# Experts of at most 64 rows: rounded rows and rests side by side in one stationary

## The chip, the cores and the metric

The kernel runs on one core of one Trainium2 chip. The metric is device time in microseconds (us), the median of three runs. Inside the core TensorE (PE) multiplies, VectorE (DVE) and ScalarE (ACT) work element by element, GpSimd (POOL) does small steps and issues the gathers and scatters, and SyncE (SP) issues nearly all other transfers (DMA).

## The reference

One layer of a hybrid encoder over 1024 tokens of width 1024: a modulated norm, a wide projection, three mixers (convolution, neighbourhood attention, a gated delta rule in both directions), an output projection, then a mixture of 32 experts, and a final norm. The change touches only the experts. Cut to what matters there:

```python
gate = pg_top * jax.nn.softmax(top_logit, axis=-1)          # two experts per token
expert = (grp[:, None] * EXPERTS_PER_GROUP + top_e).reshape(-1)
...
def expert_block(args):
    xb, e = args                                            # the rows that chose expert e
    return (jax.nn.silu(xb @ w1[e]) * (xb @ w3[e])) @ w2[e]  # 1024 -> 512, 512 -> 1024
...
ys = ys * gate...                                           # weighted, and added to the token
x = x + gate2 * y_moe
return _rmsnorm(x, final_norm_w)
```

All of it is fp32. Each expert has three weight matrices of 2 MiB each, 6 MiB together; 2048 rows (1024 tokens, two experts each) are spread unevenly over the 32 experts.

## The kernel before

**Products.** PE runs its fast fp32r form, which rounds its operands, so each fp32 operand is held as a rounded part and a rest: `split` (line 61) is one copy on ACT (the rounded part, `wh`, `xh`, `uh`) and one subtraction on DVE (the rest, `wl`, `xl`, `ul`). A product of two such operands is three matmuls in `mm3` (line 1351): rounded by rounded, rest by rounded, rounded by rest. The expert's rows are the stationary operand (128 deep, as wide as there are rows), the weights are the moving one (128 deep, 512 columns).

**Places.** The experts are ranked by size on the chip, but for the first three, which stand where they are. `ROOM` (line 30) says how many rows the expert of each rank can have; what goes beyond it is done by a loop behind the straight code (line 1611), which runs as many passes as are needed, none here. The 32 experts are taken in a fixed order of places; rank r is called a column in the code. Columns 3 and 4 (192 rows) are taken at places 18 and 24 (`TWICE`), as two blocks of 128 and 64 rows that share the weights; column 5 is at place 3, column 14 at place 12, column 19 at place 17, column 20 at place 19, column 25 at place 25, column 31 at place 31. The rooms give 128 rows at places 0 to 9, 96 at 10 to 13, 80 at 14 to 17, 64 at 19 to 23, 25 and 26, and 48 at 27 to 31. So there are 34 blocks.

**One place.** `hidden` (line 1504) makes the two hidden products: for w1 and then w3, for two halves g of the depth, it takes one weight tile of 1 MiB, split in two pieces of 128x1024 (`chunk_split`, line 1268, three buffers each for `wh` and `wl`), and runs 12 matmuls: 48 in all, in two accumulators `h1` and `h3`. `gated` (line 1382) applies Silu to the first on ACT and multiplies by the second on DVE (`u`). `prep_x` (line 1499) prepares the next place's rows: eight PE transposes into two banks `pt`, each split in `xh` and `xl`, and the gather of a later block. `output` (line 1519) multiplies the place before with its w2: 24 matmuls, two multiplications by gate and modulation into `yo` on DVE, and the scatter that adds the rows to `x2_d` (POOL). Last, `t` (line 1389) turns `u` with four PE transposes and splits it in `uh` and `ul` for the next place's turn. So a place costs 72 matmuls and 12 splits of weights. Each engine runs its instructions in order; the compiler puts them in an order of its own, near this one.

**Weights.** 192 loads of 1 MiB go through 16 buffers in order, issued by SP as buffers come free (`weights`, line 1528; `load_tile`, line 1175), with at most four in flight.

**Other lines.** `slots_of` (line 1439) finds the rows of the second blocks of columns 3 and 4, once, at place 5: 16 times DVE makes a matrix `q` (line 1455, one buffer of its own) which PE multiplies (line 1456). The last two blocks skip the scatter: their rows are put side by side (line 1558), and `out_on_chip` (line 1422) and `last` (line 1584) add them on the chip, apply the final norm and store. Line 1149 is the router's product and line 1037 one of its index steps, both true fp32 products; line 1145 is an ACT copy of a 128x512 bank.

Of the kernel before, what the change touches and what calls it, by code (L numbers as in the profile page):

```python
# [8 lines left out]
F32 = mybir.dt.float32  # L9
F32R = mybir.dt.float32r  # L10
I32 = mybir.dt.int32
AF = mybir.ActivationFunctionType
# [4 lines left out]
P = 128  # L17
# [3 lines left out]
KT = D // P  # L21
# [5 lines left out]
TWICE = (18, 24)  # L27
LATE = 5
FEATS = (*range(0, 1280, P), *range(1536, 3072, P))
ROOM = ((3, 128), (5, 192), (12, 128), (16, 96), (20, 80), (27, 64), (32, 48))  # L30


def body(tc, I, O):
# [5 lines left out]
def _body(ctx, tc, nc, I, O):  # L39
    pe, act, dve, pool, sp = nc.tensor, nc.scalar, nc.vector, nc.gpsimd, nc.sync  # L40
# [8 lines left out]
    ident = const.tile([P, P], F32, name="ident")  # L49
# [188 lines left out]
    for i in range(2):  # L238
        acc = st.tile([P, D], F32, name=f"acc{i}")
        for k in range(KT):  # L240
# [3 lines left out]
            w = st.tile([P, D], F32, name="wa", bufs=4)  # L244
# [1106 lines left out]
    def mm3(out, xh, xl, k0, w, first, last):  # L1351
        n = 0
        for k in range(4):
            wh, wl = w[k // 2]
            for a, b in ((xh, wh), (xl, wh), (xh, wl)):
                pe.matmul(out, a[:, k0 + k], b[:, k % 2], start=first and n == 0, stop=last and n == 11)  # L1356
                n += 1

    class Block:


        def __init__(self, i, idx, n=P):
            self.n = n
            self.xg, self.idx, self.yo = xgs[i % 3][:n], lambda: [x[:n] for x in idx()], None

        def gather(self):
            return pool.indirect_dma_start(out=self.xg, out_offset=None, in_=xn_d,  # L1367
# [2 lines left out]

        def x(self):
            n = self.n
            xh = ex.tile([P, KT, P], F32R, name="xh")[:, :, :n]
            xl = ex.tile([P, KT, P], F32R, name="xl")[:, :, :n]
            for g in range(2):
                pt = pse.tile([P, 4, P], F32, name="pt", bufs=2)[:, :, :n]
                for j in range(4):
                    pe.transpose(pt[:, j], self.xg[:, (4 * g + j) * P:(4 * g + j + 1) * P], ident[:n, :n])  # L1378
                split(xh[:, 4 * g:4 * g + 4], xl[:, 4 * g:4 * g + 4], pt)
            self.xs = xh, xl  # L1380

        def gated(self, n):
            if n:
                self.yo = ex.tile([P, D], F32, name="yo", bufs=2)[:self.n]
            u = self.u = self.yo[:, :512] if n else ex.tile([P, 512], F32, name="u", bufs=1)[:self.n]
            act.activation(u, self.hs[0], AF.Silu)
            dve.tensor_mul(u, self.hs[1], u)

        def t(self, n=0):
            m = self.n  # L1390
            pt = pse.tile([P, 4, P], F32, name="ut")[:, :, :m]
            for j in range(4):
                pe.transpose(pt[:, j], self.u[:, j * P:(j + 1) * P], ident[:m, :m])
            uh = ex.tile([P, 4, P >> n], F32R, name=f"uh{n}", bufs=1)[:, :, :m]
            ul = ex.tile([P, 4, P >> n], F32R, name=f"ul{n}", bufs=1)[:, :, :m]
            split(uh, ul, pt)
            self.us = uh, ul
# [41 lines left out]
    def slots_of(ebs, ob):  # L1439


        m = len(ebs)
        pb = ex.tile([P, 2, NT], F32, name="pb", bufs=1)
        dve.tensor_scalar(pb, pos, ob, None, op0=OP.add)
        sl = ex.tile([P, NT, 2, 2, 2], F32, name="sl", bufs=1)[:, :, :, :m]
        on = ex.tile([P, NT, 2], F32, name="on", bufs=1)
        for i, eb in enumerate(ebs):
            dve.tensor_scalar(on, eid, eb, None, op0=OP.is_equal)
            dve.tensor_mul(sl[:, :, :, i], slot, on[:, :, :, None].to_broadcast([P, NT, 2, 2]))
        tabo = pse.tile([P, 512], F32, name="tab")[:, :2 * m]  # L1450
        n = 0
        for t in range(NT):
            for a in range(2):
                q = ex.tile([P, P], F32, name="q", bufs=1)
                dve.tensor_scalar(q, iota, pb[:, a, t:t + 1], None, op0=OP.is_equal)
                pe.matmul(tabo, q, sl[:, t, a].rearrange("p i k -> p (i k)"), start=n == 0, stop=n == 2 * NT - 1)
                n += 1
        tb = small.tile([P, 2, 2], F32, name="tb")[:, :m]
        dve.tensor_copy(tb, tabo.rearrange("p (i k) -> p i k", k=2))
        ix1 = small.tile([P, 2], I32, name="ix1")[:, :m]  # L1460
        indices(small, tb[:, :, 0], ix1, m)
        return [(ix1[:, i:i + 1], tb[:, i, 1:2], tb[:, i, 0:1]) for i in range(m)]
# [41 lines left out]
    def hidden(bs, weights, between=iter(())):  # L1504

        for b in bs:
            b.hs = []
        for nms in (("h1", "tab"), ("h3", "y")):
            for b, nm in zip(bs, nms):
                b.hs.append(pse.tile([P, 512], F32, name=nm, bufs=2 if nm == "y" else 1)[:b.n])  # L1510
            for g in range(2):
                next(between, None)
                w = weights()
                for b in bs:
                    mm3(b.hs[-1], *b.xs, 4 * g, w, g == 0, g == 1)
        for n, b in enumerate(bs):
            b.gated(n)

# [19 lines left out]
    g = blks[0].gather()  # L1538
# [340 lines left out]
```

## Time and profile before

| | us |
|---|---|
| median of three runs | 1533.52 |
| lowest and highest run | 1529.77, 1535.05 |
| profiled execution | 1529.12 |
| span of the profile | 1527.3 |
| stretch of the experts (first hidden matmul to last) | 872.3 to 1479.5 |

Line numbers below are those of the kernel before. A matmul's time in the profile is its latency, since matmuls are pipelined; what one costs PE is the distance from start to start. On DVE and ACT, too, a short overlap of neighbours makes distances shorter than times. The busy share of an engine says how near it is to its limit in a stretch; the releaser named behind idle time says what ended a wait. PEclk is the granted clock of TensorE as a share of 2.4 GHz.

### The profile page before, as it was taken

What the parts mean: (1) busy time and instruction counts of PE and PEld (TensorE: products, weight loads), DVE (VectorE), ACT (ScalarE), POOL (GpSimd) and SP (SyncE); (2) the same over time, 40 slices, a digit from 0 to 9 for tenths busy, and PEclk for the clock granted to TensorE, in tenths of its full rate; (3) what the DMA queues carried; (4) which work ended last, traced back from release to release, by engine and by line L of the source; (5) the groups of instructions that cost most, each with busy time, mean ns of one, the idle gap of its engine ahead of it and who ended that gap; (6) DMA issues with size and microseconds to landing.
All of it is one profiled execution on the core that took longest, in us unless ns stands there. A gap on an engine that the chain in (4) does not pass through costs nothing. (4 is left out here: it accounts for less than half of the span.)

```text
span 1527.3 us, 21968 instructions
## 1 busy us (share of the span) xinstructions
PE 1380.7 (90%) x7319; PEld 1054.2 (69%) x7319; DVE 1185.0 (78%) x2148; ACT 792.4 (52%) x1293; POOL 380.9 (25%) x294
## 2 busy tenths in 40 slices
PE   3987999999877898879999699999999999999994
PEld 3865777777665888878887578787766665665542
DVE  6758766554647688867788799999999789878995
ACT  3633554433444322322322288787777567657773
POOL 0011321100101555633432111221244113212222
PEclk9999999999999999999999599999999999999997
DMA  9496455224778665677566699999999999979832
GB/s 338 120 200 195 143 183 165 88 75 96 204 208 208 187 202 181 203 252 238 207 207 226 255 335 374 346 381 364 351 374 370 363 337 371 334 271 339 322 111 117
DMA packets 172601, 375.75 MB, mean 246 GB/s; under 512 B 33458, under 2 KB 99634, under 8 KB 147908
## 3 DMA queue, kind: packets, MB, share of 16 engines
q1 hardware_dynamic: 162500, 351.13, 67.2%
q0 software_dynamic: 7072, 16.73, 4.6%
q10 hardware_dynamic: 2912, 6.46, 1.4%
q8 instruction: 59, 0.97, 0.3%
q14 instruction: 58, 0.48, 0.1%
HBM read 325.31 MB, written 56.87 MB: 250 GB/s over the span
## 5 line engine op out<-in xcount | busy, mean ns | idle before, releaser
L61 DVE TENSOR_TENSOR wl<-w,wh 128x1024 fp32r<-128x1024 f32 (+1 forms) x392 | 460.6, 1196 | 44.8 <-ACT wh L61 39.7
L61 ACT CAST wh<-w 128x1024 fp32r<-128x1024 f32 (+1 forms) x392 | 403.9, 1033 | 161.2 <-PE y L1356 69.1
L1356 PE MATMUL h<-wl,xh 128*128 128x512 f32 (+4 forms) x512 | 204.1, 399 | 0.4 <-DVE wl L61 0.3
L1356 PE MATMUL h<-wh,xh 128*128 128x512 f32 (+4 forms) x512 | 204.4, 399 | 0.1
L1356 PE MATMUL h<-wh,xl 128*128 128x512 f32 (+4 forms) x512 | 202.0, 394 | 0.6 <-DVE xl L61 0.6
L1408 POOL DMA_INDIRECT x_d<-yo,ixp x27 | 100.0, 3703 | 198.6 <-DVE yo L1404 184.1
L339 PE MATMUL mm<-hh,wh 128*128 128x512 f32 x352 | 148.1, 421 | 0.0
L339 PE MATMUL mm<-hh,wl 128*128 128x512 f32 x352 | 143.0, 406 | 1.9 <-DVE wl L61 1.9
L339 PE MATMUL mm<-hl,wh 128*128 128x512 f32 x352 | 142.6, 405 | 0.0
L1356 PE MATMUL y<-wh,uh 128*128 128x512 f32 (+4 forms) x272 | 108.8, 401 | 1.1 <-ACT uh L61 1.1
L1356 PE MATMUL y<-wl,uh 128*128 128x512 f32 (+4 forms) x272 | 108.1, 398 | 0.1
L1356 PE MATMUL y<-wh,ul 128*128 128x512 f32 (+4 forms) x272 | 106.9, 394 | 0.5 <-DVE ul L61 0.5
L1356 PEld LDWEIGHTS h<-wl,xh 128*128 128x128 f32 (+4 forms) x512 | 80.9, 158 | 36.8 <-DVE wl L61 2.0
L1356 PEld LDWEIGHTS h<-wh,xl 128*128 128x128 f32 (+4 forms) x512 | 81.0, 158 | 36.7 <-DVE xl L61 1.4
L1356 PEld LDWEIGHTS h<-wh,xh 128*128 128x128 f32 (+4 forms) x512 | 81.1, 158 | 34.2 <-ACT wh L61 0.7
L1367 POOL DMA_INDIRECT oacc<-xn_d,ixp x29 | 35.2, 1213 | 211.4 <-PE pt L1378 195.5
L339 PEld LDWEIGHTS mm<-hh,wh 128*128 128x128 f32 x352 | 68.1, 193 | 18.5 <-issue 7.0
L339 PEld LDWEIGHTS mm<-hl,wh 128*128 128x128 f32 x352 | 67.7, 192 | 15.5 <-issue 0.3
L339 PEld LDWEIGHTS mm<-hh,wl 128*128 128x128 f32 x352 | 68.1, 193 | 13.9 <-DVE wl L61 2.2
L404 POOL TENSOR_TENSOR acc<-acc,wa 128x512 f32<-128x512 f32 x28 | 41.1, 1466 | 86.3 <-ACT wa L402 47.8
L1356 PEld LDWEIGHTS y<-wl,uh 128*128 128x128 f32 (+4 forms) x272 | 42.5, 156 | 21.2 <-DVE wl L61 2.2
L1356 PEld LDWEIGHTS y<-wh,uh 128*128 128x128 f32 (+4 forms) x272 | 42.4, 156 | 19.4 <-ACT uh L61 1.6
(433 smaller groups left out, 2893.3 us busy)
## 6 DMA issues: line engine op xcount, KB each, us to landing
w<-we SPq DMA_DIRECT2D x192, 1024.0 KB
wa<-w_ada SPq DMA_DIRECT2D x64, 256.0 KB
wa<-w_ada SPq DMA_DIRECT2D x16, 512.0 KB
wr<-w_in_f SPq DMA_DIRECT2D x16, 512.0 KB
qkv_d<-t SPq DMA_DIRECT2D x12, 512.0 KB
f<-qkv_d SPq DMA_DIRECT2D x8, 768.0 KB
t_d<-zt SPq DMA_DIRECT2D x8, 516.0 KB
xt<-x SPq DMA_DIRECT2D x8, 512.0 KB
```

Source lines behind the costliest of these rows:

```text
L61: return act.copy(hi, src), dve.tensor_sub(lo, src, hi.bitcast(F32))
L339: pe.matmul(ps, a[:, k], of(b, k, h * 512, 512), start=n == 0, stop=n == 3 * KT - 1)
L404: pool.tensor_add(acc, acc, w)
L1356: pe.matmul(out, a[:, k0 + k], b[:, k % 2], start=first and n == 0, stop=last and n == 11)
L1367: return pool.indirect_dma_start(out=self.xg, out_offset=None, in_=xn_d, in_offset=bass.IndirectOffsetOnAxis(ap=self.idx()[0], axis=0), bo ...
L1408: return pool.indirect_dma_start(out=x2_d, out_offset=bass.IndirectOffsetOnAxis(ap=self.idx()[0], axis=0), in_=self.yo, in_offset=None, bo ...
```

## The change

Blocks of at most 64 rows (`both`) are computed in another way. `ROOM` now has 128 rows at places 0 to 11 and 64 at places 12 to 17, 19 to 23 and 25 to 31, so with the second blocks of places 18 and 24 there are 20 such blocks. Their rounded rows stand in columns 0 to 63 of `xh` and their rests in columns 64 to 127, as one stationary 128 wide; `mm2` multiplies it by `wh` and by `wl`, two matmuls where `mm3` has three. The accumulators then have 128 rows, of which row r and row r + 64 are to be added. `gated` only copies the two accumulators to SBUF (two ACT copies of 128x512, in a buffer of `xl`). `t` has eight true fp32 matmuls with `fold`, a 128x64 matrix of two identities above each other, which add the halves and turn the result in one step, four for each accumulator; then Silu (ACT, 128x256), the multiplication (DVE, 128x256) and the split follow on the turned rows. `su`, which holds the first two results, takes the one buffer `u`. `q` of `slots_of` takes that buffer too and loses its own.

```diff
--- before.py
+++ after.py
@@ -27,7 +27,8 @@
 TWICE = (18, 24)
 LATE = 5
 FEATS = (*range(0, 1280, P), *range(1536, 3072, P))
-ROOM = ((3, 128), (5, 192), (12, 128), (16, 96), (20, 80), (27, 64), (32, 48))
+ROOM = ((3, 128), (5, 192), (14, 128), (32, 64))
+HALF = P // 2
 
 
 def body(tc, I, O):
@@ -1356,12 +1357,25 @@
                 pe.matmul(out, a[:, k0 + k], b[:, k % 2], start=first and n == 0, stop=last and n == 11)
                 n += 1
 
+    fold = ex.tile([P, HALF], F32, name="fold", bufs=1)
+    dve.tensor_add(fold, ident[:, :HALF], ident[:, HALF:])
+
+    def mm2(out, xs, k0, w, first, last):
+
+        n = 0
+        for k in range(4):
+            for b in w[k // 2]:
+                pe.matmul(out, xs[:, k0 + k], b[:, k % 2], start=first and n == 0, stop=last and n == 7)
+                n += 1
+
     class Block:
+
 
 
         def __init__(self, i, idx, n=P):
             self.n = n
             self.xg, self.idx, self.yo = xgs[i % 3][:n], lambda: [x[:n] for x in idx()], None
+            self.both = n <= HALF
 
         def gather(self):
             return pool.indirect_dma_start(out=self.xg, out_offset=None, in_=xn_d,
@@ -1370,16 +1384,28 @@
 
         def x(self):
             n = self.n
-            xh = ex.tile([P, KT, P], F32R, name="xh")[:, :, :n]
-            xl = ex.tile([P, KT, P], F32R, name="xl")[:, :, :n]
+            xh = ex.tile([P, KT, P], F32R, name="xh")
+            if self.both:
+                self.xs = xh
+                xh, xl = xh[:, :, :n], xh[:, :, HALF:HALF + n]
+            else:
+                xh, xl = xh[:, :, :n], ex.tile([P, KT, P], F32R, name="xl")[:, :, :n]
+                self.xs = xh, xl
             for g in range(2):
                 pt = pse.tile([P, 4, P], F32, name="pt", bufs=2)[:, :, :n]
                 for j in range(4):
                     pe.transpose(pt[:, j], self.xg[:, (4 * g + j) * P:(4 * g + j + 1) * P], ident[:n, :n])
                 split(xh[:, 4 * g:4 * g + 4], xl[:, 4 * g:4 * g + 4], pt)
-            self.xs = xh, xl
+
+        def hidden(self, w, g):
+            (mm2 if self.both else mm3)(self.hs[-1], *((self.xs,) if self.both else self.xs), 4 * g, w, g == 0, g == 1)
 
         def gated(self, n):
+            if self.both:
+                self.hc = ex.tile([P, KT, P], F32, name="xl").rearrange("p (i k) f -> p i k f", i=2)
+                for i in range(2):
+                    act.copy(self.hc[:, i].rearrange("p k f -> p (k f)"), self.hs[i])
+                return
             if n:
                 self.yo = ex.tile([P, D], F32, name="yo", bufs=2)[:self.n]
             u = self.u = self.yo[:, :512] if n else ex.tile([P, 512], F32, name="u", bufs=1)[:self.n]
@@ -1388,9 +1414,20 @@
 
         def t(self, n=0):
             m = self.n
-            pt = pse.tile([P, 4, P], F32, name="ut")[:, :, :m]
-            for j in range(4):
-                pe.transpose(pt[:, j], self.u[:, j * P:(j + 1) * P], ident[:m, :m])
+            pt = pse.tile([P, 4, P], F32, name="ut")
+            if self.both:
+                ht = pt.rearrange("p k (i f) -> p i k f", i=2)
+                for i in range(2):
+                    for j in range(4):
+                        pe.matmul(ht[:, i, j], self.hc[:, i, j], fold, start=True, stop=True)
+                su = ex.tile([P, 512], F32, name="u", bufs=1).rearrange("p (i k f) -> p i k f", i=2, k=4)
+                act.activation(su[:, 0], ht[:, 0], AF.Silu)
+                dve.tensor_mul(su[:, 1], ht[:, 1], su[:, 0])
+                pt = su[:, 1][:, :, :m]
+            else:
+                pt = pt[:, :, :m]
+                for j in range(4):
+                    pe.transpose(pt[:, j], self.u[:, j * P:(j + 1) * P], ident[:m, :m])
             uh = ex.tile([P, 4, P >> n], F32R, name=f"uh{n}", bufs=1)[:, :, :m]
             ul = ex.tile([P, 4, P >> n], F32R, name=f"ul{n}", bufs=1)[:, :, :m]
             split(uh, ul, pt)
@@ -1451,7 +1488,7 @@
         n = 0
         for t in range(NT):
             for a in range(2):
-                q = ex.tile([P, P], F32, name="q", bufs=1)
+                q = ex.tile([P, 512], F32, name="u", bufs=1)[:, :P]
                 dve.tensor_scalar(q, iota, pb[:, a, t:t + 1], None, op0=OP.is_equal)
                 pe.matmul(tabo, q, sl[:, t, a].rearrange("p i k -> p (i k)"), start=n == 0, stop=n == 2 * NT - 1)
                 n += 1
@@ -1507,12 +1544,12 @@
             b.hs = []
         for nms in (("h1", "tab"), ("h3", "y")):
             for b, nm in zip(bs, nms):
-                b.hs.append(pse.tile([P, 512], F32, name=nm, bufs=2 if nm == "y" else 1)[:b.n])
+                b.hs.append(pse.tile([P, 512], F32, name=nm, bufs=2 if nm == "y" else 1)[:P if b.both else b.n])
             for g in range(2):
                 next(between, None)
                 w = weights()
                 for b in bs:
-                    mm3(b.hs[-1], *b.xs, 4 * g, w, g == 0, g == 1)
+                    b.hidden(w, g)
         for n, b in enumerate(bs):
             b.gated(n)
 
```

## Rows read from the trace of the kernel before

**Rows 1.** The page: its header and the busy time of the engines.

```profile
span 1527.3 us, 21968 instructions
...
PE 1380.7 (90%) x7319; PEld 1054.2 (69%) x7319; DVE 1185.0 (78%) x2148; ACT 792.4 (52%) x1293; POOL 380.9 (25%) x294
```

**Rows 2.** Lines view of L1386 (the Silu): count, min/median/max ns, first and last start.

```profile
L1386 ACT ACTIVATE u<-h x32: 579/586/600, 881.7 to 1475.0; 128x512 f32<-128x512 f32 x12, 64x512 f32<-64x512 f32 x7, 48x512 f32<-48x512 f32 x5, 96x512 f32<-96x512 f32 x4
L1386 ACT ACTIVATE yo<-tab x2: 585/586/587, 1208.9 to 1335.9; 64x512 f32<-64x512 f32 x2
```

**Rows 3.** Windows between Silus of places 6, 11, 17, 20, 23, 26, 31, and end.

```profile
core 0: us, PE busy (x) PEld busy (x) DVE busy (x) ACT busy (x) POOL busy (x), PEclk, DMA share, GB/s
1078.70:1184.86 106.16, 106.14 (x503) 72.13 (x502) 103.44 (x109) 84.31 (x98) 42.05 (x12) 1.00 1.00 366
1184.86:1256.49 71.63, 71.63 (x333) 46.61 (x332) 55.65 (x61) 43.13 (x53) 10.39 (x8) 1.00 0.99 351
1256.49:1311.74 55.25, 55.25 (x258) 31.64 (x257) 51.20 (x55) 42.09 (x51) 18.84 (x7) 1.00 0.99 368
1311.74:1383.38 71.64, 71.64 (x333) 45.66 (x332) 55.51 (x61) 43.08 (x52) 10.39 (x8) 1.00 0.82 283
1383.38:1475.03 91.65, 91.65 (x421) 48.44 (x420) 84.23 (x91) 68.46 (x81) 27.62 (x9) 1.00 0.68 253
1475.03:1527.30 52.27, 28.25 (x105) 13.92 (x103) 36.36 (x56) 22.32 (x32) 10.89 (x10) 0.80 0.43 164
990.00:1078.70 88.70, 88.70 (x420) 70.46 (x419) 87.13 (x91) 71.68 (x81) 18.05 (x9) 1.00 1.02 369
```

**Rows 4.** Timeline of PE, 64-row places: start us, us, engine, line.

```profile
1252.12 0.39 PE L1356 MATMUL h<-wh,xh 128*64 128x512 f32 x1
...
1253.95 0.39 PE L1356 MATMUL h<-wl,xh 128*64 128x512 f32 x1
```

**Rows 5.** Timeline of DVE near 1031 us: three weight subtractions in a row.

```profile
1031.03 3.49 DVE L61 TENSOR_TENSOR wl<-w,wh 128x1024 fp32r<-128x1024 f32 x3
```

**Rows 6.** Lines by form, 1250 to 1480 us, DVE and ACT: busy, mean ns, idle before.

```profile
L61 DVE TENSOR_TENSOR wl<-w,wh 128x1024 fp32r<-128x1024 f32 x140 | 168.4, 1217 | 24.9 <-ACT wh L61 22.8
L1404 DVE SCALAR_TENSOR_TENSOR yo<-y,tabp,oacc 64x512 f32<-64x512 f32 x14 | 10.4, 739 | 1.6 <-PE y L1356 1.6
L1387 DVE TENSOR_TENSOR u<-h,u 64x512 f32<-64x512 f32 x6 | 4.1, 675 | 0.0
L61 DVE TENSOR_TENSOR ul<-ut,uh 128x256 fp32r<-128x256 f32 x8 | 3.3, 410 | 0.4 <-ACT uh L61 0.4
...
L1386 ACT ACTIVATE u<-h 64x512 f32<-64x512 f32 x6 | 3.5, 586 | 0.0
```

**Rows 7.** Timeline of PE: true fp32 products, and four transposes of `u`.

```profile
760.01 1.87 PE L1149 MATMUL ht<-rw,hT 128*128 128x36 f32 x16
...
851.86 1.09 PE L1037 MATMUL pl<-rhs,q 128*128 128x64 f32 x4
...
1249.59 0.46 PE L1393 MATMUL ut<-ident,u 64*128 64x64 f32 x4
```

**Rows 8.** Lines by form, 700 to 870 us: an ACT copy from PSUM.

```profile
L1145 ACT COPY hT<-ht 128x512 f32<-128x512 f32 x16 | 9.4, 585 | 22.8 <-PE ht L1143 22.8
```

**Rows 9.** Timeline of DVE: `q` of slots_of and the multiplication of place 5.

```profile
960.35 0.28 DVE L1455 TENSOR_SCALAR q<-iota,pb 128x128 f32<-128x128 f32 x1
...
974.34 0.69 DVE L1387 TENSOR_TENSOR u<-h,u 128x512 f32<-128x512 f32 x1
...
979.19 0.28 DVE L1455 TENSOR_SCALAR q<-iota,pb 128x128 f32<-128x128 f32 x1
```

**Rows 10.** Waits of SP's queue, 1000 to 1480 us: total us, times, longest.

```profile
SPq L1178 <- DMA w<-we: 179.3, 75, 4.5
SPq L1178 <- DVE wl L61: 151.7, 70, 5.6
```

**Rows 11.** Windows, columns as in rows 3: the start of the experts.

```profile
850.00:900.00 50.00, 39.01 (x171) 31.79 (x171) 41.46 (x167) 26.30 (x41) 6.05 (x5) 0.75 0.75 287
```

## The prediction

> **What bounds the kernel now.** I read the page first. PE is busy 90% of the span and DVE 78% [rows 1]; such shares are means over stages with different limits, so the next view is a cut at the experts. The Silu of each block marks the places, 34 in all [rows 2], and windows between them give each group of places its own line [rows 3]. There are five of interest, 396.3 us together: A, places 12 to 17, 106.16 us, 17.7 each; B, 18 to 20, 71.63; C, 21 to 23, 55.25, 18.4 each; D, 24 to 26, 71.64; E, 27 to 31, 91.65, 18.3 each. In all of them PE is busy for the whole window at a granted clock of 1.00, so PE's queue sets the pace. Three things in the same lines matter as much. DVE is busy 103.4 of 106.2 us in A, 51.2 of 55.3 in C and 84.2 of 91.7 in E: it is right behind PE. In B and D, where two blocks share the weights, it has room (55.65 of 71.63). The DMA engines are at 0.99 to 1.00 up to 1311 us and fall to 0.68 and 0.82 later.
>
> What a matmul costs is read from distances: eight starts lie in 1252.12 to 1253.95, so 0.229 us each [rows 4], though its latency stands at 0.39.
>
> **PE's side.** Each of the 20 blocks loses 16 of its 48 hidden matmuls: 16 x 0.229 = 3.66 us. The stationary gets 128 wide instead of 48 to 80; places 7 to 11, mostly of 128 rows, take 88.70/5 = 17.7 us [rows 3], no more than the narrow ones, so the wider load hides behind the matmul before it. Eight true fp32 matmuls with 64 columns come in, four transposes go, which took 0.4 us to the next matmul [rows 7]. The trace bounds a fp32 product: 16 with 36 columns took 1.87 us, 0.12 each, and 4 with 64 columns 1.09 us, 0.27 each, these at the end of the router, where the granted clock is low [rows 7, 11]. I take 0.20, between the wider form and the faster clock: 8 x 0.20 - 0.4 = 1.2 us added (0.5 to 1.8). So PE saves 2.46 us per block, and a place of 64 rows would need 18.42 - 2.46 = 15.96 us.
>
> The Trainium skill bears on this price: "FP8 and Floating Point Precision", section TensorE Precision Notes, says that true fp32 takes four passes through the array. 4 x 64 columns at 2.4 GHz are 0.107 us by an estimate from that page, so 0.5 us added per block and PE at 15.3; no row here shows 64 columns at the full clock, and the sum goes without it.
>
> **DVE's side.** Here the saving ends. A place has 12 subtractions of 128x1024, 1.217 us each [rows 6]; in a row they follow at (3.49 - 1.217)/2 = 1.135 [rows 5], 0.08 less than the time of one, and I take that overlap off the others too. After the change: 12 x 1.135 + 2 xl x 0.33 + multiplication 0.33 + ul 0.33 + 2 yo x 0.66 = 16.26 us. The change takes only 0.27 off, since the multiplication shrinks from 675 ns to the 410 of a 128x256 form [rows 6]; the weight splits, 13.6 of it, are not touched. So in single places DVE, not PE, is late next. It can run nearly full: in places 7 to 11 it was busy for 87.13 of 88.70 us [rows 3], 98%. 16.26/0.98 = 16.6; I take 16.7 (16.3 to 17.8). The three buffers of wh and wl let DVE be three pieces ahead, which evens out hidden phases (DVE longer) against output phases (PE longer).
>
> **ACT's side.** Two copies of 128x512 from PSUM, 0.585 each by the router's copy [rows 8], and a Silu of half the width replace one Silu of 0.586 [rows 6]: about +0.95 us. In C ACT is busy 42.09 us, 14.0 per place [rows 3]; 15.0 of 16.7 still fits, with less room.
>
> **The sums by stage.** A: 6 x 16.7 = 100.2, -6.0. C: 3 x 16.7 and 0.5 for the 128 rows of place 24 = 50.6, -4.6. E: 5 x 16.7 = 83.5, -8.1. B and D are PE's: 71.6 less three hidden products (11.0), plus three turns (3.6) = 64.2, and 1 for the places in them where DVE is late: 65.2, -6.4 each. Together -31.5.
>
> Against that: places 10 and 11 get 128 rows instead of 96. A DVE subtraction grows by 1.05 ns a column (410 ns at 256 columns, 1217 at 1024 [rows 6]), so three of them by 128 columns cost 0.4 us a place; some of the 0.8 hides: +0.5 (0 to 0.8). The matrices q now share the buffer u. Before, they stood around place 5's own multiplication, which came between two of them, and the last 14 took from 960.35 to 979.19 us [rows 9]. With one buffer in program order, all 16 lie between the transposes of place 4 and Silu of place 5, which frees the accumulators for place 6; behind the waiting Silu the ACT queue holds place 6's weight copies. Nothing to 8 us; I take +3, since each step waits for PE in turn but the weights between can be moved. At the end, nothing hides the longer turn of the last block: its fp32 products, Silu, multiplication and split come in sequence ahead of the last output product: +1.5 (0 to 3). The gathers and scatters stay; invalid rows move nothing. Rows that leave their room would go to the loop, but the reference's router with its own inputs gives 58, 52, 52, 51, 51, 51 rows to ranks 14 to 19 and fewer behind, 79 and 76 to ranks 12 and 13.
>
> Sum: -31.5 + 5 = -26.5 us. Against the profiled execution, 1529.12 us with a span of 1527.3, that is 1502.6; that execution lies 4.4 below the median of 1533.52, from which the sum gives 1507. I say 1505.
>
> **Rivals.**
> The hand-over chain. Before, u went ACT, DVE, PE, ACT, DVE, with one crossing behind the transposes. Now Silu, multiplication, rounding and subtraction cross four times behind them, in engines that run in order. With one weight subtraction (1.2 us) ahead of the multiplication, ACT stands still behind its Silu for up to 1.6 us and delays the weight roundings for which DVE waits (22.8 us of that are there already [rows 6]). At 17.8 us per single place A gives +0.6, C -1.3, E -2.6; with B and D -16.1, with the +5 -11: 1522. For it: DVE has no slack to make good a wait. Against it: ACT's 1.7 us of room.
>
> The weights. Six places are 36 MiB, 37.7 MB, and in A the DMA engines moved 366 GB/s at a share of 1.00 [rows 3], some 0.5 MB a place of it gathers and scatters: 18.5 us per expert. Without a stock 20 experts would take 370 us, -26, and with the +5 -21: 1512. Against it: there are 16 buffers, and SP waited 151.7 us for a buffer to come free, nearly as long as for arrivals, 179.3 [rows 10]; A eats 6 x 1.8 = 11 us of a stock of up to 49, and B and D, with 21.7 us per expert, refill it.
>
> DVE without loss. Products at 0.12, places at 16.3, no cost of q and tail: about -42, 1491.
>
> Slower: the clock. Now PE is never idle among the experts. If it waits for DVE in every place, PE is busy 96% at 15.96 of 16.7 us, in short gaps, and the clock may be taken to its lower level, 1.2 GHz, for a part of the time. PE's work in the five stages would be 396.3 - 20 x 2.46 = 347 us; it decides from a mean granted clock of 347/391 = 0.89 down. At 0.85 it takes 408 us: +17 with the +5, 1550. For it: at 850 to 900 us, with PE busy 39 of 50 us, the clock was 0.75 [rows 11]. Against it: that is much more idle time than 4%.
> The Trainium skill, "TensorE: Matmul & The Clock Gate", section A second HAM failure mode: psum-queue depth-cycling, holds that frequent short idle moments between groups of matmuls let the clock swing between its two levels. By that rule this rival would come true; the trace shows no such case at such small gaps, so it keeps a small chance.
>
> **Chances.** Forecast (1495 to 1515) 0.62; chain 0.17; weights 0.07; DVE without loss 0.06; slower clock, or rows that go to the loop after all, 0.08. The range reaches from DVE without loss, taken from the profiled execution (1488), to the chain with a dearer q and tail (1526). The measurement can tell about 0.3%, 4.6 us, from no change: faster 0.86, the same 0.06 (the end of the chain's spread), slower 0.08.
>
> **What would show it.** mm2's distances stay at 0.229 us and `fold` lies below 0.27. Single places take 16.3 to 17 us with DVE busy 97% or more and PE below 97%; B and D take 64 to 66 with PE full. If PE stays full in A, C and E at the new pace, DVE's floor is wrong; if places stay near 18 with DVE waiting for wh, it is the chain; if DVE waits for w and DMA is at 1.00 up to the end, it is the weights; if PEclk falls below 0.95 in A to E, it is the clock. In place 5 the Silu would come after the last q. The prediction is wrong altogether if the order in which the engines' work is put changes much.

## The result, and the profile after

The changed kernel takes 1516.46 us (median of 4 runs, 1514.39 to 1518.59), the kernel before 1531.83 beside it (4 runs, 1529.77 to 1535.05): a ratio of 0.9898, 95% interval 0.9873 to 0.9923. It is faster, by about 15 us or 1.0%; the forecast was 26 to 28. The profiled execution took 1518.59 us.

The page of the changed kernel, header and busy time of the engines:

```profile
span 1516.8 us, 21838 instructions
...
PE 1355.5 (89%) x7239; PEld 1076.5 (71%) x7239; DVE 1173.4 (77%) x2143; ACT 804.9 (53%) x1333; POOL 424.2 (28%) x294
```

Against [rows 1] the span is only 10.5 us shorter. A part of the comparison is chance: the experts begin at 889.2 us here and at 881.7 in [rows 2], though nothing ahead of them was changed but the making of `fold`, one addition of 0.22 us. In the twelve other kernels below this start lies between 878.6 and 888.2. The start is the first Silu, in the changed kernel:

```profile
L1412 ACT ACTIVATE u<-h x14: 583/587/598, 889.2 to 1331.1; 128x512 f32<-128x512 f32 x14
```

So I compare from the first place to the end and call this stretch "the experts": 645.6 us before, 627.6 after, -18.0.

The windows of the changed kernel between the same marks as in [rows 3] (in small blocks the first copy of `h` by ACT, L1407, stands where the Silu stood); columns as there. First places 7 to 11, then A, B, C, D, E and the end; the last line is one single place, 15:

```profile
997.94:1087.43 89.49, 89.49 (x422) 72.68 (x421) 87.66 (x91) 72.75 (x82) 21.58 (x10) 1.00 1.01 368
1087.43:1192.35 104.92, 100.67 (x477) 69.95 (x476) 98.85 (x109) 86.72 (x108) 45.56 (x12) 1.00 1.00 370
1192.35:1259.39 67.04, 66.88 (x334) 49.38 (x333) 54.72 (x63) 45.03 (x60) 15.51 (x8) 1.00 1.01 368
1259.39:1311.08 51.69, 49.83 (x234) 33.26 (x233) 48.88 (x53) 43.69 (x55) 27.73 (x7) 1.00 1.01 385
1311.08:1378.07 66.99, 66.83 (x334) 49.37 (x333) 54.72 (x63) 45.03 (x60) 16.64 (x9) 1.00 0.89 306
1378.07:1465.52 87.45, 81.78 (x383) 54.19 (x381) 82.70 (x96) 70.66 (x88) 41.07 (x8) 1.00 0.71 265
1465.52:1516.80 51.28, 27.08 (x112) 15.89 (x111) 35.92 (x50) 23.84 (x34) 13.40 (x11) 0.81 0.44 167
1139.65:1157.18 17.53, 16.91 (x82) 11.13 (x81) 16.41 (x19) 14.50 (x19) 10.53 (x3) 1.00 1.02 396
```

Against [rows 3], forecast and measured:

| stretch | before | after | change | forecast |
|---|---|---|---|---|
| places 5 and 6 (the matrices q) | 41.0 | 41.6 | +0.6 | +3 |
| places 7 to 11 | 88.7 | 89.5 | +0.8 | +0.5 |
| A | 106.2 | 104.9 | -1.2 | -6.0 |
| B | 71.6 | 67.0 | -4.6 | -6.4 |
| C | 55.3 | 51.7 | -3.6 | -4.6 |
| D | 71.6 | 67.0 | -4.6 | -6.4 |
| E | 91.7 | 87.5 | -4.2 | -8.1 |
| end | 52.3 | 51.3 | -1.0 | +1.5 |

The stages of single places (A, C, E) hold most of the shortfall: 9.7 of 13.3 us in the five stages. There PE is no longer full and DVE isn't either. The place from 1139.65 stands for them: places 13 to 16 take 17.53 to 17.58 us. It is DVE's 16.41 us of work and 1.12 us in which DVE stands still. Where that is, the timeline of the same place shows (start, duration, engine, line; PE, then ACT, then DVE):

```profile
1140.28 0.66 PE L1422 MATMUL ut<-fold,xl 128*128 128x64 f32 x4
1140.75 0.48 PE L1368 MATMUL h<-wl,xh 128*128 128x512 f32 x1
...
1141.76 0.55 PE L1422 MATMUL ut<-fold,xl 128*128 128x64 f32 x4
...
1143.14 0.39 PE L1357 MATMUL y<-wh,uh 128*64 128x512 f32 x1
...
1144.38 0.71 PE L1397 MATMUL pt<-ident,oacc 64*128 64x64 f32 x8
1145.13 0.44 PE L1357 MATMUL y<-wh,uh 128*64 128x512 f32 x1
...
1150.25 1.00 PE L1422 MATMUL ut<-fold,xl 128*128 128x64 f32 x8
1151.06 0.48 PE L1368 MATMUL h<-wh,xh 128*128 128x512 f32 x1
...
1160.67 0.39 PE L1357 MATMUL y<-wh,uh 128*64 128x512 f32 x1
...
1142.87 2.21 ACT L62 CAST wh<-w 128x1024 fp32r<-128x1024 f32 x2 [0.32 <-PE h L1368]
...
1146.54 1.05 ACT L62 CAST wh<-w 128x1024 fp32r<-128x1024 f32 x1 [0.43 <-PE y L1357]
...
1151.28 0.39 ACT L1424 ACTIVATE u<-ut 128x256 f32<-128x256 f32 x1
...
1143.01 3.49 DVE L62 TENSOR_TENSOR wl<-w,wh 128x1024 fp32r<-128x1024 f32 x3
1147.62 1.23 DVE L62 TENSOR_TENSOR wl<-w,wh 128x1024 fp32r<-128x1024 f32 x1 [1.12 <-ACT wh L62]
...
1153.83 0.41 DVE L62 TENSOR_TENSOR ul<-u,uh 128x256 fp32r<-128x256 f32 x1
```

And the waits of 1104.5 to 1192.35 us, five single places (total us, times, longest):

```profile
PEld h L1368 <- DVE wl L62: 10.8, 19, 0.7
ACT wh L62 <- PE h L1368: 8.4, 23, 0.4
DVE wl L62 <- ACT wh L62: 5.6, 5, 1.2
ACT wh L62 <- PE y L1357: 5.0, 14, 0.5
ACT wh L62 <- DMA w<-we: 0.8, 2, 0.5
```

Read together: while the hidden products run, PE waits for DVE's next `wl`, some four times a place. Two output products stand among the hidden ones, the first at 1143.14; where they begin in a row (1145.13), the three buffers of `wh` are full; ACT can round the next piece only when the first piece's products are done (1146.54), and DVE waits for that from 1146.50 to 1147.62, once in every place. So a place has two stretches with different owners, DVE in the hidden one and PE in the output one, and neither engine makes up in one what it loses in the other. The counts give a reason, which the experiments put to the test: the change takes a hidden piece from six products to four, 0.92 us by [rows 4], under DVE's 1.135 [rows 5], and leaves an output piece at six, 1.4 us, over it. Before, all pieces had six.

### The profile page after: what moved, and what is told of

The parts are those of the page before. It is cut to its first block, busy times and chain, and to the rows that moved or that the text cites. A ratio compares the mean times of both kernels' runs of the same rounds, so it can differ in the third digit from the quotient of the medians.

```text
span 1516.8 us, 21838 instructions
## 1 busy us (share of the span) xinstructions
PE 1355.5 (89%) x7239; PEld 1076.5 (71%) x7239; DVE 1173.4 (77%) x2143; ACT 804.9 (53%) x1333; POOL 424.2 (28%) x294
## 5 line engine op out<-in xcount | busy, mean ns | idle before, releaser
L1445 POOL DMA_INDIRECT x_d<-yo,ixp x27 | 127.0, 4704 | 222.8 <-DVE yo L1441 214.4
L1368 PE MATMUL h<-wl,xh 128*128 128x512 f32 x288 | 122.8, 427 | 9.0 <-DVE wl L62 7.9
L1368 PE MATMUL h<-wh,xh 128*128 128x512 f32 x288 | 113.3, 401 | 0.7 <-ACT wh L62 0.7
L1357 PE MATMUL y<-wh,uh 128*64 128x512 f32 (+1 forms) x272 | 108.2, 398 | 0.8 <-ACT uh L62 0.5
L1357 PE MATMUL y<-wh,ul 128*64 128x512 f32 (+1 forms) x272 | 107.1, 394 | 0.4 <-DVE ul L62 0.4
L1357 PE MATMUL y<-wl,uh 128*64 128x512 f32 (+1 forms) x272 | 106.3, 398 | 0.7 <-DVE wl L62 0.7
L1357 PE MATMUL h<-wh,xh 128*128 128x512 f32 x224 | 90.3, 403 | 1.0 <-ACT u L1412 0.9
L1357 PE MATMUL h<-wl,xh 128*128 128x512 f32 x224 | 89.6, 400 | 0.0
L1357 PE MATMUL h<-wh,xl 128*128 128x512 f32 x224 | 88.5, 395 | 0.8 <-DVE xl L62 0.6
L1368 PEld LDWEIGHTS h<-wl,xh 128*128 128x128 f32 x288 | 54.3, 189 | 40.3 <-DVE wl L62 31.6
L340 PEld LDWEIGHTS mm<-hh,wh 128*128 128x128 f32 x352 | 68.2, 194 | 18.2 <-issue 6.9
L1368 PEld LDWEIGHTS h<-wh,xh 128*128 128x128 f32 x288 | 54.4, 189 | 8.8 <-ACT wh L62 1.4
L1357 PEld LDWEIGHTS y<-wl,uh 128*64 128x64 f32 (+1 forms) x272 | 42.6, 157 | 20.9 <-DVE wl L62 2.4
```

Of the source, the lines that this page charges most:

```text
L340: pe.matmul(ps, a[:, k], of(b, k, h * 512, 512), start=n == 0, stop=n == 3 * KT - 1)
L1368: pe.matmul(out, xs[:, k0 + k], b[:, k % 2], start=first and n == 0, stop=last and n == 7)
L1445: return pool.indirect_dma_start(out=x2_d, out_offset=bass.IndirectOffsetOnAxis(ap=self.idx()[0], axis=0), in_=self.yo, in_offset=None, bo ...
```

## The experiments

The theory under test is this **loop**: in a single place PE's and DVE's time both count, each for a part. Its rivals: DVE's own floor (the place would follow DVE alone), the hand-overs of the turn, and matters beside it (rooms, q, weights). It took shape during the runs. For e1 to e4 the theories were "buffers" (DVE stops because the buffers of `wh` are full, and that alone is lost), "DVE floor", "turn" (PE alone) and "weights"; e6, e7 and e9 to e12 were set against the loop. For place 15 the windows give this, worked out as place less DVE busy:

| kernel | place | DVE busy | DVE still |
|---|---|---|---|
| changed kernel | 17.53 | 16.41 | 1.12 |
| e1 four buffers | 18.10 | 16.61 | 1.49 |
| e3 turn in fp32r | 17.06 | 16.43 | 0.63 |
| e4 one `wl` less | 16.80 | 15.49 | 1.31 |
| e7 turn twice | 18.79 | 16.67 | 2.12 |
| e9 halves between | 17.04 | 16.36 | 0.68 |
| e10 both e3 and e9 | 16.87 | 16.35 | 0.52 |
| e12 e3, `ul` on POOL | 16.69 | 16.30 | 0.39 |

**e1, four buffers of wh and wl** (a weight buffer given up for the room), and **e2**, its control.

```diff
-    WA, WX, WB = 5, 3, 8
+    WA, WX, WB = 4, 3, 8          # e1 and e2
-    exw = ctx.enter_context(tc.tile_pool(name="exw", bufs=3))
+    exw = ctx.enter_context(tc.tile_pool(name="exw", bufs=4))   # e1 alone
```

> The changed kernel with four buffers each for the pieces wh and wl instead of three, room for them made by one weight buffer less (15 instead of 16). In the changed kernel a place with a single block of 64 rows takes 17.53 us, with DVE busy 16.4 of it and PE waiting 2.2 us for wl in the hidden product. Theory buffers: DVE stands 1.1 us per place because all three wh are held by the output product, and that is what PE lacks in the hidden product; with a fourth buffer single places take 16.4 to 16.8 us and the kernel 1502 to 1508 us. Theory DVE floor: 17.5 us is what DVE's queue takes with its handovers, nothing moves. Theory turn: the fp32 products cost PE what it gained, nothing moves. Theory weights: transfers set 17.5 us, and with one weight buffer less it gets no better or worse.

> The changed kernel with 15 weight buffers instead of 16 and nothing else, the control for the fourth wh and wl. Theories buffers, DVE floor and turn: no difference from the changed kernel, 1516 us within 3. Theory weights: a smaller stock ends earlier, DVE and ACT wait for w, single places over 17.8 us.

e2 took 1516.93 us (ratio 0.992, 0.9891 to 0.9949), as the changed kernel: the sixteenth weight buffer is worth nothing. e1 took 1521.07 (0.9941, 0.992 to 0.9962). The expected gain did not come; places 13 to 16 take 18.1 to 18.2. Its waits from 1105 to 1175 us, four places:

```profile
PEld h L1368 <- DVE wl L62: 7.5, 12, 0.9
PEld h L1368 <- ACT wh L62: 4.4, 4, 1.1
DVE yo L1441 <- PE y L1357: 3.4, 8, 0.5
DVE u L1425 <- ACT u L1424: 2.0, 4, 0.5
```

DVE's wait for `wh` is gone, as the theory has it, but the order in which the engines' work is put came out differently: DVE now waits for results (`yo`, `u`), and PE for ACT's roundings. The run says that this stop of DVE hung on the buffers; it doesn't say what a fourth would bring in the old order. In the same run places 30 and 31, in yet another order, take 17.05. So the order in which the compiler puts the work decides as much as the buffers do, and no run here varies it alone with four of them.

**e3, the turn in fp32r.** The hidden result loses its rests before it is turned, so this kernel computes a little less exactly.

```diff
-    fold = ex.tile([P, HALF], F32, name="fold", bufs=1)
+    fold = ex.tile([P, HALF], F32R, name="fold", bufs=1)
-                self.hc = ex.tile([P, KT, P], F32, name="xl").rearrange(...
+                self.hc = ex.tile([P, KT, P], F32R, name="xl").rearrange(...
```

> The changed kernel with the eight products by fold in the fast fp32r form, whose operands are rounded, instead of true fp32: the hidden result loses its rests. This takes about 1 us of PE time off each of the 20 blocks. Theory turn (PE is the bound in single places): 1.0 us per place, together about 20 us, 1497. Theories buffers and DVE floor: in single places the time goes to waiting for wl, under 0.3 us each; only the two groups with shared weights, where PE is full, lose 3 us each: 1507 to 1513.

1500.52 us (0.9809, 0.9782 to 0.9837), the fastest of all; its experts take 615.7 us, 11.9 less than in the changed kernel. A single place of e3, and the second half of its turn with the product behind it:

```profile
1132.33:1149.39 17.06, 16.02 (x74) 10.23 (x73) 16.43 (x19) 14.60 (x20) 9.87 (x3) 1.00 1.02 393
```

```profile
1142.44 0.53 PE L1422 MATMUL ut<-fold,xl 128*128 128x64 f32 x4
1142.81 0.48 PE L1368 MATMUL h<-wh,xh 128*128 128x512 f32 x1
```

DVE has the same work as in the changed kernel and still the place is 0.47 shorter, because PE's turn is: its eight products take 0.75 us of the place instead of 1.64, and they are no work of DVE's. DVE's floor alone is refuted. So is PE alone: 0.47 lies between the 1.0 of "turn" and the 0.3 at most of the other theories, and the time, too, is in neither range.

**e4, one wl of twelve left out** in 18 single places (the products read `wh` twice instead, so a rest of the weights is missing from the result).

```diff
+            if skip and k0:
+                act.copy(wh, w[:, k0:k0 + 2])
+                parts.append((wh, wh))
+                continue
```

> The changed kernel with one of the twelve subtractions for wl left out in the 18 single places of 64 rows: in the last piece of w3, wh is multiplied twice and the rest is missing. It takes 1.13 us off DVE in the hidden product and leaves PE's work as it is. Theories buffers and DVE floor: single places become 0.9 to 1.1 us shorter (16.4 to 16.6), the kernel 12 to 18 us: 1498 to 1504. Theory turn or weights: nothing moves.

1509.34 us (0.9862, 0.9834 to 0.989), the experts 623.1, 4.5 less than in the changed kernel, where 12 to 18 was expected. A single place of e4:

```profile
1135.89:1152.69 16.80, 16.42 (x82) 11.20 (x81) 15.49 (x18) 14.41 (x20) 5.71 (x3) 1.00 1.02 407
```

In A a place fell to 16.80, by 0.73 for 0.92 of DVE's work. In E, where the order of the work came out differently, three places took 18.4 to 18.9, and E lost 2.0 us.

**e7, the turn's products done twice**, PE's work alone.

```diff
-                for i in range(2):
+                for i in (0, 0, 1, 1):
```

> The changed kernel with each of the eight products by fold done twice, into the same place: 1.9 us of PE per block, twice its cost. Rounded products instead of true ones (1.0 us less per block) took 0.5 us off a single place and 2.4 off each group with shared weights. Theory loop (part of the products lies where PE waits for wl anyway): single places +0.6 to +1.2 us, B and D +4 to +6 each, together +18 to +28: 1534 to 1544. Theory that PE's queue alone sets the pace: +1.9 us per block, +38: 1554. Theory DVE floor: single places unchanged, B and D +5 each: 1526.

1539.51 us (1.0073, 1.0049 to 1.0097), inside the loop's range and outside the others', though a place grew a little more than the loop's 0.6 to 1.2. A single place of e7:

```profile
1136.21:1155.00 18.79, 18.46 (x98) 13.22 (x97) 16.67 (x19) 14.63 (x19) 3.19 (x2) 1.00 1.02 409
```

1.8 us more for PE, 1.26 more for the place, with DVE still for 2.12. So PE's time counts for some 0.5 (e3, 0.47 of 0.9) to 0.7 (e7), and DVE's for 0.8 (e4, in A). Were one engine the bound, one of the two would count in full and the other for nothing.

**e5, the new rooms alone on the kernel before, and e6, the change without them** in A and just ahead of it (blocks of 96 and 80 rows keep the old passes there).

```diff
-ROOM = ((3, 128), (5, 192), (12, 128), (16, 96), (20, 80), (27, 64), (32, 48))
+ROOM = ((3, 128), (5, 192), (14, 128), (32, 64))                       # e5, on before
-ROOM = ((3, 128), (5, 192), (14, 128), (32, 64))
+ROOM = ((3, 128), (5, 192), (12, 128), (16, 96), (20, 80), (32, 64))   # e6, on after
```

> The kernel before with the new rooms and nothing else: places 10 and 11 get 128 rows, 12 to 17 get 64, 27 to 31 get 64, all with three matmuls per product. The forecast prices the rooms at +0.5 us. Theory that the gain comes from two matmuls instead of three: stage A within 2 us of before (its turn and split on DVE get shorter, PE's matmuls stay), all else the same, 1529 to 1535. Theory that part of the gain is the rooms' (narrower blocks in A, DVE has less to do): 3 us or more faster.

> The changed kernel with the old rooms of 96 and 80 rows at places 10 to 17, so these keep three matmuls; the 14 blocks of places 18 to 31 keep the change. In the changed kernel stage A took 104.9 us against 106.2 before. If single places of 64 rows gain nothing over 80 or 96 rows in the old way (theory loop: DVE sets the hidden stretch, PE the output and turn), it is 1 to 2 us slower than the changed kernel, 1517 to 1520. By the forecast (single places at 16.7) it would be 6 slower, 1522.

e5 took 1530.66 us (1.0017, 1.0004 to 1.003), so the rooms cost 2 to 3 us by themselves. In part they cost it in A: with 64 rows in the old way places 15 and 16 take 18.5 us, where with 80 rows they took 17.3 and 17.6. e6 took 1511.95 (0.9879, 0.9856 to 0.9903), and its experts 628.1 us against 627.6: A stands at 106.1 there against 104.9, places 7 to 11 at 88.6 against 89.5. For the blocks of 96 and 80 rows the two passes with their smaller rooms gain as good as nothing; what the change brings, it brings where blocks had 64 or 48 rows, and where single places took 18.3 to 18.4 us before, not 17.7. The profiled total of e6 is the lower one only by what lies ahead of the experts (883.0 us against 889.2).

**e8, a buffer of its own for q** (one run; a weight buffer given up for the room, as in e2).

```diff
-                q = ex.tile([P, 512], F32, name="u", bufs=1)[:, :P]
+                q = ex.tile([P, P], F32, name="q", bufs=1)
```

> The changed kernel with a buffer of its own for q again, room for it made by one weight buffer less (15, which by its control costs nothing). The stretch from place 4 to place 6, in which all 16 steps of q stand, took 41.0 us before and 41.6 in the changed kernel. The forecast put +3 (0 to 8) on the shared buffer; if the trace's 0.6 is that price, the stretch goes back to 41.0 and the Silu of place 5 comes before the last q again; nothing else moves.

1516.74 us; places 5 and 6 take 41.0 again, as before. So the shared buffer costs 0.6 us.

**e9, the output products in two halves between the hidden pieces**: w1, first half of y, w3, second half; the same instructions in another order, the loads too. **e10** joins it with e3; **e11** puts the order on the kernel before.

```diff
+            if nms[0] == "h1":
+                mid()                       # output(places_[p - 1], weights, 0)
...
-            output(places_[p - 1], weights)
+            output(places_[p - 1], weights, 1)
```

> Edit on the changed kernel: the output product of the block before is put between the hidden pieces in two halves (w1, first half of y, w3, second half of y) instead of both halves behind all hidden pieces; the loads of the weights follow the same new order. Nothing is added or left out, the same instructions in another order. Theory (a place is a loop of two stretches with different owners: hidden pieces paced by DVE's weight subtractions, then output products and turn paced by PE while DVE stands still because its three wh/wl buffers are held): shorter stretches mean that three buffers bridge them, so single places go from 17.53 to 16.4 to 16.9 us, A to 99 to 102, C to 49 to 50.5, E to 83 to 85, in all -8 to -14 us against the changed kernel: 1502 to 1508. Rival 1 (DVE's own work with its gaps is the floor, the place takes 17.5 whatever the order): no change within 3 us, 1514 to 1519. Rival 2 (the turn's chain of hand-overs at the end of a place is what costs): the chain is as long as before, 17.3 to 17.6 a place, 1512 to 1519.

> The order of e9_inter together with the fp32r turn of e3_fold_r (the eight products that add the halves and turn them take fp32r, so that the hidden result loses its rests before it is turned). Theory (loop): the two gains overlap, since the fp32r turn shortens the stretch paced by PE and the new order bridges it: single places at DVE's 16.3 to 16.6 us, doubles as in e3_fold_r (B 64.6), 1490 to 1500. Rival 1 (DVE's floor at 17.05 as e3_fold_r has it): as e3_fold_r, 1499 to 1503. Rival 2 (turn's chain): e3_fold_r's 1500.5 as well.

> Control: the order of e9_inter put on the kernel before, whose places of one block are full of PE work. Theory (loop): there PE never waits for long, so the order has nothing to give: within 3 us of the kernel before, 1527 to 1534. If the order helped for another reason than the loop (loads that arrive earlier, fewer conflicts of DMA), it would help here too: -8 or more.

e9 took 1511.86 us (0.9892, 0.9862 to 0.9921), e10 1504.97 (0.9862, 0.9841 to 0.9883), e11 1526.03 (0.9984, 0.9969 to 1.0). A single place of e9, and one of e10:

```profile
1131.80:1148.84 17.04, 16.30 (x82) 11.39 (x81) 16.36 (x19) 14.59 (x20) 4.97 (x2) 1.00 1.02 397
```

```profile
1127.85:1144.72 16.87, 15.33 (x73) 10.49 (x72) 16.35 (x19) 14.35 (x20) 11.16 (x3) 1.00 1.02 399
```

The order alone takes DVE's stop from 1.12 to 0.68, and A from 104.9 to 101.7; with e3's shorter turn to 0.52. The two gains overlap (0.49, 0.47, together 0.66), as the loop has it. But the size fell short of the 16.4 to 16.9 expected of e9, and in all nothing is left: places 7 to 11, whose blocks are full and which needed no such order, take 1.3 more, the end 4.8 more, and the last three places of E take 17.5, 18.0 and 18.5. Rivals 1 and 2 have the total (0.9892 against the changed kernel's 0.9898) and not the places. e10, too, is no gain on e3: its experts take 618.7 us against 615.7. The control e11 gained 2.3 us of its experts where 0 was expected, 0.7 of it in A, so of e9's -3.2 in A some 0.7 has another reason than the loop.

What e3, e4 and e7 show is that both engines' times count in a single place and that neither alone is the bound. That the three buffers couple them rests on the waits and on e1, where the order changed as well.

Most of the longer end can be read from the traces. In the changed kernel output products of place 30 stand behind the last turn and cover it, and PE waits 0.90 us; in e9 that half has gone ahead, nothing covers the turn, and PE waits 2.86. The products of the changed kernel that end the wait come first, then those of e9 and the window behind them:

```profile
1477.31 0.45 PE L1357 MATMUL y<-wh,uh 128*64 128x512 f32 x1 [0.49 <-ACT uh L62]
1478.16 0.44 PE L1357 MATMUL y<-wh,ul 128*64 128x512 f32 x1 [0.41 <-DVE ul L62]
```

```profile
1466.91 0.67 PE L1358 MATMUL y<-wh,uh 128*64 128x512 f32 x2 [1.71 <-ACT uh L62]
1468.73 0.69 PE L1358 MATMUL y<-wh,ul 128*64 128x512 f32 x1 [1.15 <-DVE ul L62]
```

```profile
1470.00:1475.00 5.00, 5.00 (x14) 2.67 (x13) 1.97 (x2) 1.49 (x2) 0.00 (x0) 0.53 0.00 0
```

Behind the wait the granted clock of e9 is 0.53, near the lower level of 1.2 GHz, and twelve distances are 0.43 us instead of 0.23. The wait and the slow products make some 4.4 of the 4.8 us.

**e12, e3 with ul made on POOL**, to take work off DVE.

```diff
-            split(uh, ul, pt)
+            if self.both:
+                act.copy(uh, pt)
+                pool.tensor_sub(ul, pt, uh.bitcast(F32))
+            else:
+                split(uh, ul, pt)
```

> e3_fold_r (turn in fp32r, the hidden result loses its rests before it is turned) with the subtraction that makes ul moved from DVE to POOL in the 20 small blocks. It takes 0.33 us (estimate from the 410 ns of a 128x256 subtraction less 0.08 of overlap) off DVE in each; POOL will take about 0.73 (half of the 1455 ns of its 128x512 sums), off the path, since ul is wanted only by the output product, a whole hidden stretch later. Theory (a single place is a loop in which DVE's time counts for a part: leaving out 1.135 of DVE's work in e4_skip_wl took 0.75 off a place): -0.2 us a place, 17.05 to 16.8 or 16.9, DVE busy 16.1 of it; -3 to -5 us against e3_fold_r: 1495 to 1498. Rival 1 (DVE's time counts in full): -0.33 in all 20 blocks, 16.7 a place, -6 us or more: 1494 or less. Rival 2 (POOL's subtraction comes behind a scatter of 6.3 us in POOL's queue and the output product waits for ul, or it slows DVE's own subtractions): PE waits for ul, places of 17.2 us or more: 1503 and over.

1513.47 us (0.9897, 0.9874 to 0.992), 13 more than e3. The windows of e12: a single place, and three stretches of place 21, the first after B (columns as before):

```profile
1133.30:1150.00 16.70, 15.78 (x73) 10.26 (x74) 16.31 (x18) 14.60 (x19) 10.55 (x4) 1.00 0.99 378
...
1254.00:1258.00 4.00, 1.02 (x5) 0.64 (x6) 2.00 (x2) 1.23 (x2) 3.67 (x3) 1.00 1.02 432
1258.00:1261.50 3.50, 3.50 (x11) 1.81 (x10) 1.87 (x2) 2.40 (x4) 0.09 (x1) 0.54 1.03 397
1261.50:1266.00 4.50, 4.16 (x20) 2.65 (x18) 3.13 (x5) 3.38 (x5) 0.88 (x1) 0.97 0.97 400
```

The waits of e12 from 1245 to 1271 us:

```profile
POOL x_d L1449 <- DVE wl L62: 10.5, 1, 10.5
PEld y L1357 <- POOL ul L1435: 3.5, 1, 3.5
```

Both happened. Single places fell by 0.36 to 16.70, more than the loop's 0.2. But DVE's busy time fell only by 0.13, since a weight subtraction ran longer in most places: of the 60 in places 13 to 17, the four that began while POOL made `ul` took 1.42 to 1.94 us, the others 1.20 to 1.23 as in e3. The rest came off DVE's stop. So rival 1's size is there, and its reason can't be read from this run. Rival 2 decided the total: where `ul` stands in POOL's queue behind a scatter that is itself waiting (10.5 us here) and no hidden stretch covers it, the output products wait for `ul`. Place 21 took 20.6 us against 16.1 in e3. The end took 57.7 against 50.8: PE waits there 2.98 us for `ul` and 1.80 for a late `wl`, and the granted clock is 0.69 from 1460 to 1465 us and 0.82 from 1475 to 1480, where e3 has 1.00.

## Why the prediction was right in sign and too large

**The step that failed is the single place.** I took 16.26/0.98 and then 16.7 us, with the words that three buffers even out hidden phases against output phases. It measured 17.53. DVE's floor itself held (16.41 busy against 16.26). The 98% came from places 7 to 11, where every piece has six products and DVE stays behind PE at one even pace; after the change pieces have four or six, DVE is late in one stretch and stopped in the other, and the buffers are too few to bridge it: 1.12 us still where the step allowed 0.44. With A, C and E this step carries 9.7 of the 13.3 us. Among the runs only e12, with a shorter turn and less for DVE to do, brings a place to the 16.7 that I had forecast.

**Luck.** The five stages missed by 13.3 us, the experts by only 8.5 (-18.0 for -26.5), because the +5 that I put against them for q, rooms and end came to +0.4. That these errors are opposite has no reason in the prediction.

**PE's price held.** The distances of mm2 stay at 0.23 us. A product of the turn stands in the trace as two records; the sixteen make up 1.64 us of a single place, 0.205 for each of the eight products, and 0.20 was taken. In B, 0.6 of the missing 1.8 us is the turn (24 products took 5.2 us, 4.2 net of the transposes, where I took 3.6); the hidden products of the single blocks there follow at 0.263 us on the mean over 63 distances, with a median of 0.234: 1.8 us, where I had put 1 for places in which DVE is late. The Trainium skill's "FP8 and Floating Point Precision", section TensorE Precision Notes, states four passes for true fp32, which would be 0.107 us by an estimate from that page; the trace decides for 0.205.

**q** was sized too dear: all sixteen went ahead of place 5's Silu, as forecast, and that Silu began 34.0 us behind the one of place 4 instead of 19.4. But the weight copies went ahead of it, and PE waited 0.91 us for it, once. Timeline of DVE and ACT in the changed kernel, last q and Silu, against [rows 9]:

```profile
989.36 0.28 DVE L1492 TENSOR_SCALAR u<-iota,pb 128x128 f32<-128x128 f32 x1
...
990.34 0.59 ACT L1412 ACTIVATE u<-h 128x512 f32<-128x512 f32 x1
```

**The end** came out at -1.0 where I had +1.5: the last window begins in the middle of the last place, and I left out that its second half loses eight hidden products, 8 x 0.229 = 1.8 us. Nor is the last turn uncovered: output products of place 30 stand behind it, and PE waits 0.90 us for `uh` and `ul` where it waited 1.58 before. **The rooms** cost what was said, +0.8 in places 7 to 11; alone on the kernel before (e5) they cost 2 to 3 us.

**The rivals.** By the time the weights (1512) come nearest, by the place the chain (17.8 us; 1522), and its sign, DVE waiting for `wh`, is there; but its mechanism isn't. ACT doesn't stand behind its Silu in these places, it waits for PE to let go of `wh`; and `ul`, the last of the turn, is done at 1154.24 us, 6.4 before the first product with `uh` at 1160.67. The weights were no bound: ACT waited 0.8 us for them in five places, and leaving a buffer out (e2) changed nothing. SP waited 159.0 us for arrivals and 151.5 for buffers, much as in [rows 10]. The clock stayed at 1.00 in all of A to E, with waits of PE of up to 0.7 us in four hidden pieces of every place. The Trainium skill's rule on frequent short idle moments ("TensorE: Matmul & The Clock Gate", section A second HAM failure mode: psum-queue depth-cycling) is not borne out by stops of this length.

## What to carry to other kernels

Where an engine feeds another through a few buffers, don't divide one engine's sum over a whole pass by a share read elsewhere: work out the pace of both engines piece by piece, stretch by stretch, and ask where each will stand still. If the products per piece differ between stretches, both engines' times count in part, and the sum of the longer one is a floor, not a forecast. And an engine that has room (POOL here) may still be the wrong place for work, if its queue holds a long transfer just where nothing covers the wait.

## What the runs showed of the hardware beside this

A true fp32 product of 64 columns stands in the trace as two records, in fp32r (e3) as one. Four of them in a row take 0.81 us to the next product in the changed kernel (1150.25 to 1151.06) and 0.37 in e3 (1142.44 to 1142.81), so true fp32 costs a little over twice as much.

In e12 POOL's subtraction and DVE's weight subtractions hold each other up. In place 15 they stand so:

```profile
1136.21 1.25 POOL L1435 TENSOR_TENSOR ul<-u,uh 128x256 fp32r<-128x256 f32 x1
1137.09 3.74 DVE L62 TENSOR_TENSOR wl<-w,wh 128x1024 fp32r<-128x1024 f32 x3
```

Three weight subtractions take 3.74 us instead of 3.49 [rows 5]. In places 13 to 17 the four that began beside POOL's all ended 1.09 us after POOL was done, however early they had begun. Twice in E it is the other way round: five weight subtractions in a row take 1.21 us each, and POOL's beside them takes 6.5. The subtractions that make the rests of the rows (`xh<-pt,xh`, with one operand in PSUM) take 0.42 us beside POOL as in e3 without it.

In place 21 of e12 PE was busy for 1.02 of 4 us, and in the 3.5 us after it the granted clock was 0.54, near the lower level of 1.2 GHz; the output products then followed at 0.43 us instead of 0.23 for seven distances, and the clock was back at 0.97 in the next window. Two of them in PE's timeline:

```profile
1258.90 0.63 PE L1357 MATMUL y<-wl,uh 128*64 128x512 f32 x1
1259.33 0.63 PE L1357 MATMUL y<-wh,uh 128*64 128x512 f32 x1
```

So this stop cost some 7 x 0.2 = 1.4 us more than itself: the slower clock that I had as a rival exists, but not for the stops of this change.

The stretch ahead of the experts varies between executions of the same work: its end stands at 889.2 us in the changed kernel's profile and at 883.0 and 883.3 in those of e6 and e7, which change nothing there. A difference of two profiles in their whole span is no measure of a change of this size; a cut at the stage is.
